# Sums of the mixes over two units instead of one, placed ahead of z, and three loads issued one unit sooner

## The chip, the cores and the metric

The kernel runs on one core of a Trainium2 chip. The metric is the device time in microseconds; lower is better. Times of the program are medians of several runs; the profile is one further execution.

## The reference, cut to what matters

```python
x_prev[:, 1:, :] = x[:, :-1, :]                 # x is (16, 2048, 256) fp32
xv = x * time_mix_v + x_prev * (1 - time_mix_v)
xr = x * time_mix_r + x_prev * (1 - time_mix_r)
v = xv.reshape(-1, 256) @ value_weight
r = xr.reshape(-1, 256) @ receptance_weight
out = (sigmoid(r) * v) @ output_weight          # (16, 2048, 256) fp32
```

The reference computes a key product too, but its output does not depend on it, and the kernel leaves it out. The weights are scaled with the time mixes beforehand, so that a mix is x + c * x_prev: one product with a coefficient per channel (`c_sb`) and one sum.

## The kernel before

**Units and pieces.** The 32,768 tokens are cut into 64 units of 512 tokens, four to a batch. A unit g is worked on with its channels on the partitions, as 1,024 elements per partition (two halves of the 256 channels, called ko 0 and ko 1, times 512 tokens). `pieces(u)` gives the two mixes of unit u: m = 0 for the receptance r, m = 1 for the value v. Tiles `mix` hold two units (an even one and the odd one behind it) with both mixes; there are three such tiles in turn.

**A loop over g.** The order on every engine is the order of the program text; nothing is reordered. In one pass for unit g:

- TensorE projects r of unit g into `psum_r` (`project`, L364, 4 matmuls), transposes tokens of a later unit as long as there are any (L269; from unit 34 on the transposed tokens come by DMA), projects v of unit g into `psum_v` (L364), and multiplies an earlier z with the output weight (L393, 8 matmuls). From unit 34 on the output of unit g - 2 stands between r and v; before, that of g - 1 stands behind v. `psum_v` has one buffer, so v of unit g + 1 waits until z of unit g has read it.
- ScalarE takes the sigmoid of r (L629), copies transposed tokens (L286) and outputs (L442), and from unit 34 on makes a part of the products (`scale_act`, L609).
- VectorE makes products (`scale`, L334), sums (`add`, L356), z = sigmoid * v (L668) and, once in four units, a shifted copy at the border of a batch (`wrap_slots`, L528).
- GpSimd makes the other half of the products (`scale_pool`, L344). By a dependency written by hand it starts only when the last sum of the list `sums[g]` has ended. It also issues the loads of x.

**Lists.** What is mixed when is written down ahead of the loop in lists by unit: `products[g]` ahead of the sums, `sums[g]` ahead of v and z, `held[g]` behind z, and `pooled[g]` for GpSimd, behind `sums[g]`. From unit 10 on (`PAIRS`) the products cover two units at once: ko 0 by VectorE at `products[w]` (or, for m = 1 from unit 34 on, by ScalarE one unit sooner), ko 1 by GpSimd at `pooled[w - 1]`, with w = u - 2 for m = 0 and w = u - 1 for m = 1, u being the even unit of the pair. The sums, however, are made unit by unit: of unit u, that of m = 0 is in `held[u - 2]` (from unit 8 on) and that of m = 1 in `sums[u - 1]`.

**Loads and stores.** The last six batches are cast to bf16 in DRAM by a load that GpSimd issues (`load`, L155 and L159) and then transposed by a DMA on SyncE's queue (`by_dma`, L251), three batches at a time, at units 27 and 39. `STAGE_AT` says in which unit loads 13, 14 and 15 are issued, behind GpSimd's product; each waits by hand for the transposition that was issued at unit 27. The transposition at unit 39 waits for these loads, and the stores of some units wait in SyncE's queue for them (`FIRST`, `WAITING`).

Of the kernel before, what the change touches and what calls it, by code (L numbers as in the profile page):

```python
# [15 lines left out]
def kernel(  # L16
# [32 lines left out]
    TU = UJ * P  # L49
# [12 lines left out]
    FIRST = {21: 27, 27: 39, 29: 39}  # L62
    WAITING = {23: 27, 25: 27, 31: 39, 33: 39, 35: 39}
    ZEROS_AT = 12
    STAGE_AT = {33: 13, 34: 14, 35: 15}
    GROUPS = [(2, 3), (4, 5, 6), (7, 8, 9), (10, 11, 12), (13, 14, 15)]
    HALVED = (12, 15)
    PAD = 16
# [4 lines left out]
    PAIRS = 10  # L73
# [63 lines left out]
    def zero_rows(b, k):  # L137
        rows = zeros[k * PAD : (k + 1) * PAD].rearrange("p (o c) -> p o c", o=1)
        nc.gpsimd.dma_start(
            out=x_both[b][k, :PAD].rearrange("p (h c) -> p h c", c=P),  # L140
            in_=rows.to_broadcast([PAD, KO, P]),
        )

    def load(b):
        if b < STAGED:
            x_bf[b] = xpool.tile([P, J, D], BF16, name="x_bf")
        if b < BYUNIT:
            for e in range(UB):
                nc.gpsimd.dma_start(
                    out=x_bf[b][:, e * UJ : (e + 1) * UJ, :], in_=unit_rows(x, b, e)[:, 0]  # L150
                )
            return
        if b in HALVED:
            return [
                nc.gpsimd.dma_start(out=x_bf[b][:, j : j + J // 2], in_=rows(b)[:, j : j + J // 2])  # L155
                for j in (0, J // 2)
            ]
        run = 8192 if b < LONG else 16384
        return nc.gpsimd.dma_start(out=x_bf[b], in_=rows(b), max_dma_last_dim=run)  # L159
# [339 lines left out]
    def tile_for(b):  # L499

        if b not in mix:
            mix[b] = mixpool.tile([P, 2, 2 * UJ, KO, P], BF16, name="mix")

    def pieces(g):

        b, e = divmod(g, UB)
        tile_for(g // 2)
        return [(b, m, e * TU, (e + 1) * TU) for m in range(2)]
# [68 lines left out]
    sums = {g: [] for g in range(-1, NU)}  # L577
# [4 lines left out]
    first = {}  # L582
    held[0].append(pieces(1)[1])
    pooled[0].append(pieces(1)[1])
    for u in range(2, NU):
        p0, p1 = pieces(u)
        if u - 1 <= AHEAD:
            sums[u - 1].append(p0)
        else:
            held[u - 2].append(p0)  # L590
        (held if u - 1 < AHEAD else sums)[u - 1].append(p1)
        first[u] = (u - 1 if u - 1 <= AHEAD else u - 2, u - 1)
# [24 lines left out]
    for g in range(NU - 1):  # L617
# [48 lines left out]
        n = TU // 2 if g == NU - 2 else TU  # L666
# [10 lines left out]
        if ZEROS_AT <= g < ZEROS_AT + len(pads):  # L677
            zero_rows(*pads[g - ZEROS_AT])
        if g in STAGE_AT:
            b = STAGE_AT[g]  # L680
            loads[b] = load(b)
# [40 lines left out]
```

## Time and profile before

| | |
|---|---|
| median of 3 runs | 200.42 us (200.24 to 200.9) |
| profiled execution, its own time | 201.01 us |
| span of the profile (first to last instruction) | 199.2 us |
| TensorE busy, of the span | 192.5 us, 97% |
| VectorE busy | 184.4 us, 93% |
| ScalarE busy | 177.0 us, 89% |
| GpSimd busy | 86.9 us, 44% |
| granted TensorE clock | 0.995 |

In the profile PE is TensorE's matmuls, PEld its weight loads, DVE VectorE, ACT ScalarE, POOL GpSimd and SP SyncE; a small q behind a name means the engine's queue, which issues DMAs. L356 is line 356 of the kernel. A row of the timeline gives start, duration, engine, line, operation, output and inputs, shapes and count; neighbouring equal instructions are merged into one row. In brackets stands how long the engine was idle before, and for whom.

Two successive VectorE rows overlap by about 0.08 us[...]. The distance from start to start, which is called the step below, is therefore what an instruction takes from the engine when the next one is ready.

### The profile page before, as it was taken

The page shows a single profiled execution, that of the slowest core. Times are in us where ns is not written, and L with a number is a line of the kernel's source. Part 1 is how long each engine was busy: PE and PEld are TensorE (multiplying, and loading weights), DVE is VectorE, ACT ScalarE, POOL GpSimd, SP SyncE. Part 2 cuts the span into 40 slices and gives each one's busy share as a digit, 9 for nine tenths or more (in the row PEclk, how much of TensorE's full clock was granted, in tenths as well). Part 3 has the DMA queues.
Part 4 walks back from the last instruction along what each step waited for, and adds up shares of the span by engine and source line. Part 5 has one row for each costly group of instructions (what it writes and reads, how often), then busy time and mean ns, then how long its engine had stood idle before and what let it go on. Part 6 is the DMA issues. An engine that isn't in the chain of part 4 may idle for free.

```text
span 199.2 us, 3758 instructions
## 1 busy us (share of the span) xinstructions
PE 192.5 (97%) x1368; PEld 123.5 (62%) x1368; DVE 184.4 (93%) x289; ACT 177.0 (89%) x197; POOL 86.9 (44%) x115
## 2 busy tenths in 40 slices
PE   8999999999999999999999999999999999999990
PEld 3555676666666666666666556666666666666660
DVE  0899999999999999999999999999999999999960
ACT  3699899999999999999999999999999999999970
POOL 1656452453675635524424366444444444444200
PEclk9999999999999999999999999999999999999998
DMA  5799999999999999999999999999999999999994
GB/s 177 203 187 215 215 280 275 278 282 274 286 312 332 285 285 331 296 268 211 296 250 290 367 276 207 209 280 295 198 238 346 416 421 400 409 399 407 409 392 177
DMA packets 37961, 58.13 MB, mean 292 GB/s; under 512 B 26068, under 2 KB 27448, under 8 KB 35128
## 3 DMA queue, kind: packets, MB, share of 16 engines
q1 hardware_dynamic: 33392, 41.34, 60.7%
q0 software_dynamic: 4400, 16.44, 41.6%
q8 instruction: 10, 0.16, 0.3%
q10 hardware_dynamic: 152, 0.13, 0.2%
q14 instruction: 7, 0.06, 0.1%
HBM read 34.34 MB, written 39.90 MB: 373 GB/s over the span
## 4 chain that ended last, share of the span: by engine, by line
PE 88%; ACT 4%; DMA 2%; issue 2%; DVE 1%; SPq 0%; DVEq 0%
PE psum_v L364 26%; PE psum_o L393 26%; PE psum_r L364 26%; PE ps_t L269 8%; DMA w_f<-n_receptance_weight_dram 2%; ACT xt_first L286 1%; ACT s_sb L629 1%; PE psum_r L378 1%; PE ps_t L393 1%; ACT mix L609 1%; ACT o_sb L442 1%; PE ps_t L364 0%; SPq L171 0%; DVE z_sb L668 0%; DVE mix L356 0%
## 5 line engine op out<-in xcount | busy, mean ns | idle before, releaser
L344 POOL TENSOR_SCALAR mix<-xt_both,c_sb 128x1024 bf16<-128x1024 bf16 (+1 forms) x55 | 61.3, 1114 | 84.7 <-DVE mix L356 82.8
L356 DVE TENSOR_TENSOR mix<-mix,xt_both 128x1024 bf16<-128x1024 bf16 x112 | 77.4, 701 | 1.4
L668 DVE TENSOR_TENSOR z_sb<-s_sb,psum_v 128x1024 bf16<-128x1024 bf16 (+1 forms) x64 | 76.7, 1200 | 1.9 <-PE psum_v L364 0.8
L364 PEld LDWEIGHTS <-w_bf 128*128 128x128 bf16 x516 | 49.0, 98 | 38.7 <-DVE mix L356 0.5
L629 ACT ACTIVATE s_sb<-psum_r 128x1024 bf16<-128x1024 f32 x63 | 65.2, 1035 | 6.2 <-PE psum_r L364 6.0
L364 PE MATMUL psum_v<-mix,w_bf 128*128 128x512 bf16 (+1 forms) x256 | 65.3, 377 | 0.1
L364 PE MATMUL psum_r<-mix,w_bf 128*128 128x512 bf16 (+1 forms) x252 | 64.2, 377 | 0.0
L393 PE MATMUL psum_o<-wo_bf,z_sb 128*128 128x256 bf16 x486 | 63.4, 273 | 0.2 <-DVE z_sb L668 0.2
L393 PEld LDWEIGHTS <-z_sb 128*128 128x128 bf16 x512 | 51.7, 103 | 18.2 <-DVE z_sb L481 0.7
L442 ACT COPY o_sb<-psum_o 128x1024 f32<-128x1024 f32 x50 | 51.2, 1024 | 5.0 <-PE psum_o L393 5.0
L286 ACT COPY xt_both<-ps_t 128x1024 bf16<-128x1024 bf16 x32 | 32.8, 1036 | 0.0
L269 PEld LDWEIGHTS <-x_bf 128*128 128x128 bf16 x304 | 19.7, 98 | 8.9 <-DMA x_bf<-in_x_dram 1.5
L269 PE MATMUL ps_t<-ident,x_bf 128*128 128x128 bf16 x304 | 22.7, 219 | 0.3 <-DMA x_bf<-in_x_dram 0.3
L334 DVE TENSOR_SCALAR mix<-xt_both,c_sb 128x1024 bf16<-128x1024 bf16 (+1 forms) x47 | 21.1, 458 | 0.0
L609 ACT ACTIVATE mix<-xt_both,c_sb 128x1024 bf16<-128x1024 bf16 x14 | 16.3, 1161 | 0.0
L356 DVE TENSOR_TENSOR mix<-mix,xt_first 128x1024 bf16<-128x1024 bf16 x15 | 10.6, 713 | 0.1
L442 ACT COPY x_bf<-psum_o 128x1024 f32<-128x1024 f32 x10 | 10.2, 1015 | 0.0
L334 DVE TENSOR_SCALAR mix<-xt_first,c_sb 128x512 bf16<-128x512 bf16 x22 | 6.5, 348 | 0.3 <-ACT xt_first L279 0.2
L286 ACT COPY xt_first<-ps_t 128x1024 bf16<-128x1024 bf16 x6 | 6.2, 1027 | 0.0
L159 POOL DMA_DIRECT2D x_bf<-in_x_dram x8 | 5.7, 712 | 0.0
L528 POOL COPY xt_first<-xt_first 128x254 bf16<-128x254 bf16 x5 | 2.0, 395 | 6.6 <-DVE mix L356 6.6
L344 POOL TENSOR_SCALAR mix<-xt_first,c_sb 128x512 bf16<-128x512 bf16 x6 | 4.1, 689 | 0.7 <-DVE mix L356 0.2
(70 smaller groups left out, 54.0 us busy)
## 6 DMA issues: line engine op xcount, KB each, us to landing
out_dram<-o_sb SPq DMA_DIRECT2D x24, 1024.0 KB, 14.1
x_bf<-in_x_dram POOLq DMA_DIRECT2D x8, 1024.0 KB, 20.6
x_natural<-in_x_dram POOLq DMA_DIRECT2D x4, 1024.0 KB, 13.3
out_dram<-x_bf SPq DMA_DIRECT2D x4, 1024.0 KB, 13.1
x_natural<-in_x_dram POOLq DMA_DIRECT2D x4, 512.0 KB, 15.2
x_bf<-in_x_dram POOLq DMA_DIRECT2D x6, 256.0 KB, 6.1
out_dram<-x_bf SPq DMA_DIRECT2D x6, 256.0 KB, 4.2
o_sb<-in_x_dram SPq DMA_DIRECT2D x4, 256.0 KB, 4.0
```

The source lines that it names most:

```text
L159: return nc.gpsimd.dma_start(out=x_bf[b], in_=rows(b), max_dma_last_dim=run)
L269: nc.tensor.transpose(out=ps[:, jj], in_=src[:, jj, ko * P : (ko + 1) * P], identity=idn)
L286: nc.scalar.copy(out=xt[b][:, j0 : j0 + UJ], in_=ps)
L334: nc.vector.tensor_scalar(out=mixed(piece)[:, :, ko], in0=tokens(piece, 0, ko), scalar1=c_sb[:, m, ko : ko + 1], scalar2=None, op0=ALU.mult,)
L344: op = nc.gpsimd.tensor_scalar(out=mixed(piece)[:, :, 1], in0=tokens(piece, 0, 1), scalar1=c_sb[:, m, 1:2], scalar2=1.0, op0=ALU.mult, op1 ...
L356: return nc.vector.tensor_tensor(out=mixed(piece), in0=mixed(piece), in1=tokens(piece, 1), op=ALU.add)
L364: nc.tensor.matmul(out=ps[:, mo, :], lhsT=w_bf[:, m, ko, mo * P : (mo + 1) * P], rhs=mixed((b, m, e * TU + lo, e * TU + hi))[:, :, ko], st ...
L393: nc.tensor.matmul(out=ps[:, j, :], lhsT=slot[:, ko, j], rhs=wo_bf[:, ko, :], start=(ko == 0), stop=(ko == KO - 1),)
L442: nc.scalar.copy(out=o[:, j0 : j0 + UJ, :], in_=ps)
L609: nc.scalar.activation(out=mixed(piece)[:, :, ko], in_=tokens(piece, 0, ko), func=ACT.Copy, scale=c_sb[:, m, ko : ko + 1],)
L629: nc.scalar.activation(out=s_sb, in_=ps_r, func=ACT.Sigmoid)
L668: nc.vector.tensor_tensor(out=z_sb[:, :, c : c + n], in0=s_sb[:, :, c : c + n], in1=ps_v[:, :, c : c + n], op=ALU.mult,)
```

## The change

The sums of m = 0 and of m = 1 are made for both units of a pair in one instruction each, 2,048 elements per partition in place of 1,024, from unit 10 on. For a pair with even unit u, that of m = 0 moves to `sums[u - 2]` and that of m = 1 to `sums[u - 1]`; both stand ahead of z, and nothing is put into `held` any more. The products keep their places. Loads 13, 14 and 15 are issued in units 32, 33 and 34.

```diff
-    STAGE_AT = {33: 13, 34: 14, 35: 15}
+    STAGE_AT = {32: 13, 33: 14, 34: 15}
...
     for u in range(2, NU):
         p0, p1 = pieces(u)
+        if u >= PAIRS:
+            if u % 2 == 0:
+                for n, (b, m, lo, hi) in ((2, p0), (1, p1)):
+                    sums[u - n].append((b, m, lo, hi + TU))
+            first[u] = (u - 2, u - 1)
+            continue
         if u - 1 <= AHEAD:
             sums[u - 1].append(p0)
         else:
             held[u - 2].append(p0)
         (held if u - 1 < AHEAD else sums)[u - 1].append(p1)
         first[u] = (u - 1 if u - 1 <= AHEAD else u - 2, u - 1)
```

## The prediction

> **What bounds the kernel now.** I read the page first, then the waits, then the timeline of single engines around the units that the change touches.
>
> ```profile
> PE 192.5 (97%) x1368; PEld 123.5 (62%) x1368; DVE 184.4 (93%) x289; ACT 177.0 (89%) x197; POOL 86.9 (44%) x115
> ...
> PE   8999999999999999999999999999999999999990
> ...
> DVE  0899999999999999999999999999999999999960
> ```
>
> TensorE is busy in every slice but the first and the last. The table of stretches gives it 70.00 of the 70 us from 42 to 112 and 75.00 of the 75 from 112 to 187, and the chain of waits puts 88% of the span on PE. Its pace is that of the matmuls: 8 output matmuls take 0.87 us in the chain, and the middle units (to 33) repeat every 3.05 us, the late ones (from 34) every 2.60, three times 0.87. So VectorE, though 93% busy, can give nothing back by being shorter. It can only take: v of the next unit needs z of this one out of `psum_v`. What counts is how late z runs.
>
> ```profile
> DVE z_sb L668 <- PE psum_v L364: 0.8, 4, 0.2
> ```
>
> In the list of waits, z has waited only 0.8 us for v in all. By the timeline z starts 0.11 us after v's modelled end at the earliest (that is z on time); the bound for lateness I read at unit 6, where z ran until 32.82 and v of unit 7 started at 32.87, the only place between units 5 and 33 where it slipped (by 0.11 us). So v may start 0.05 us behind z's end. Late units then allow a z that is 0.2 us later than on time (2.60 - 1.03 for v - 1.22 for z - 0.05 - 0.11 = 0.19), middle ones 0.64.
>
> **Unit 8, where the double sums begin.** VectorE's rows:
>
> ```profile
> 34.73 1.22 DVE L668 TENSOR_TENSOR z_sb<-s_sb,psum_v 128x1024 bf16<-128x1024 bf16 x1
> 35.86 0.79 DVE L356 TENSOR_TENSOR mix<-mix,xt_both 128x1024 bf16<-128x1024 bf16 x1
> 36.57 1.00 DVE L334 TENSOR_SCALAR mix<-xt_both,c_sb 128x512 bf16<-128x512 bf16 x3
> 37.49 0.68 DVE L356 TENSOR_TENSOR mix<-mix,xt_both 128x1024 bf16<-128x1024 bf16 x1
> 38.10 1.21 DVE L668 TENSOR_TENSOR z_sb<-s_sb,psum_v 128x1024 bf16<-128x1024 bf16 x1
> 39.23 0.70 DVE L356 TENSOR_TENSOR mix<-mix,xt_both 128x1024 bf16<-128x1024 bf16 x1
> ...
> 39.98 0.47 DVE L334 TENSOR_SCALAR mix<-xt_both,c_sb 128x1024 bf16<-128x1024 bf16 x1
> 40.56 0.69 DVE L356 TENSOR_TENSOR mix<-mix,xt_both 128x1024 bf16<-128x1024 bf16 x1
> ```
>
> and TensorE's v of units 8 and 9:
>
> ```profile
> 36.36 1.03 PE L364 MATMUL psum_v<-mix,w_bf 128*128 128x512 bf16 x4
> ...
> 39.41 1.03 PE L364 MATMUL psum_v<-mix,w_bf 128*128 128x512 bf16 x4
> ```
>
> VectorE has no gap here: z of unit 8 (38.10) is already 0.6 us later than on time, ends at 39.31, and v of unit 9 starts at 39.41. Only 0.05 us is left. The row at 37.49 is the m = 1 sum of unit 9; the row at 39.23, behind z, is the m = 0 sum of unit 10, which the change doubles and puts ahead of z. The last two rows show a second thing: a sum that reads the product just ahead of it starts 0.10 us after that product's end (40.56 against 39.98 + 0.475), not 0.08 before it.
>
> **The skill on the two operations.** "VectorE: DVE Perf Modes", section "The perf-mode tier table", gives 1,224 ns to a tensor_tensor of 2,048 bf16 elements in SBUF; the same page says that an instruction's fixed cost is paid once per instruction. The trace has no such row, but its sum of 1,024 takes 0.68 us with a step of 0.60. Two steps without any saving are 1.21; I take 1.22 us of duration and, 0.08 less as in the other rows, a step of 1.13 (bounds 1.13 to 1.21). The saving is 0.07 us a pair, not half an instruction. "SBUF — State Buffer", section "Who interferes with whom", says that VectorE and GpSimd share a port pair, and that whoever has it blocks the other for the whole instruction. The trace agrees:
>
> ```profile
> 81.29 1.13 DVE L356 TENSOR_TENSOR mix<-mix,xt_both 128x1024 bf16<-128x1024 bf16 x1
> ...
> 80.75 1.13 POOL L344 TENSOR_SCALAR mix<-xt_both,c_sb 128x1024 bf16<-128x1024 bf16 x1
> ```
>
> GpSimd ended at 81.88, the sum at 82.42, 0.54 later; the sum at 35.86 also ended 0.54 after GpSimd (36.11). So a blocked sum has 0.14 of its 0.68 us behind it and does the rest when GpSimd is done. For a blocked product of 0.475 I estimate 0.335 after GpSimd. The forecast goes by the trace's numbers.
>
> **Part 1: 108 single sums become 54 double ones.** They occupy 54 x (2 x 0.60 - 1.13) = 4 us less of VectorE. Worth to the end: nothing, since TensorE sets it.
>
> **Part 2: the order at unit 8.** A step of 1.13 goes in ahead of z: 38.10 becomes 39.23, z ends at 40.45, v of unit 9 starts at 40.50 instead of 39.41: 1.1 us lost. Queued behind that v are output 8 and everything TensorE does later, with no idle time to win it back. With the other end of the step it is 1.2. At unit 9 VectorE does z 1.13, border copy 0.14, product 0.48, gap 0.10, double sum 1.13: 2.98 a unit, under 3.05, so unit 10 starts without another wait, though barely.
>
> **Part 3: the middle units.** Each has z 1.13, product 0.48, gap 0.10, double sum 1.13 = 2.84 us, in every fourth unit 0.14 more, against 3.05. VectorE catches up by unit 14. Cost 0; what hides it is the 0.21 us by which TensorE is slower.
>
> **Part 4: the late units.** Now every sum starts behind a GpSimd product that itself waits for the sum before it; in the kernel before, the sum held behind z filled that time.
>
> ```profile
> 118.92 1.22 DVE L668 TENSOR_TENSOR z_sb<-s_sb,psum_v 128x1024 bf16<-128x1024 bf16 x1
> ...
> 121.09 0.68 DVE L356 TENSOR_TENSOR mix<-mix,xt_both 128x1024 bf16<-128x1024 bf16 x1
> ...
> 119.12 1.12 POOL L344 TENSOR_SCALAR mix<-xt_both,c_sb 128x1024 bf16<-128x1024 bf16 x1 [0.80 <-DVE mix L356]
> ...
> 121.87 1.12 POOL L344 TENSOR_SCALAR mix<-xt_both,c_sb 128x1024 bf16<-128x1024 bf16 x1 [0.58 <-DVE mix L356]
> ```
>
> GpSimd follows the sum's end by 0.17 us in odd units (118.95 to 119.12) and 0.10 in even ones (121.77 to 121.87), and takes 1.12. One pair, from the start of the m = 1 sum in an odd unit (0): it ends at 1.22; GpSimd's m = 0 product runs 1.39 to 2.51. z starts at 1.13, and VectorE's product could start at 2.26, but is blocked, and ends at 2.51 + 0.335 = 2.84. The m = 0 double sum follows at 2.94, ends at 4.16; GpSimd's m = 1 product runs 4.26 to 5.38; the next m = 1 sum needs it and starts 0.04 later (a sum at 69.10 began 0.02 after GpSimd's end; others 0.09): 5.42. TensorE needs 5.20. The allowed lateness of 0.2 is spent where the pace drops at unit 34, since VectorE needs 2.84 there. From unit 35 to 61 there are 13 pairs: 13 x 0.22 = 2.9 us. Without the blocking the product ends at 2.74 and the round is 5.32: 13 x 0.12 = 1.5. ScalarE's part of the m = 1 product ends earlier than GpSimd's and costs nothing.
>
> **Part 5: the loads.** Four DMA issues (0.56, 0.56 and two in 1.10 us on GpSimd) move up one unit. Load 13 goes behind GpSimd's product at unit 32 (110.49 to 111.61); the transposition it waits for landed at 110.61, so it need not wait, and there is 1.8 us of cover before the product at 113.94. Load 15's 1.10 us fit between two products (1.4 us). In SyncE's queue the held stores and the second transposition (133.90 to 151.13) come up to 2.6 us sooner, but GpSimd first needs its result at 155.45. Beside the two stores at 110.70 the loads may land later; those 4.3 us cover it. Cost and gain 0.
>
> **Sum.** 1.1 + 2.9 = 4.0 us: span 199.2 to 203.2, the profiled execution, which lies 1.8 over its span and 0.6 over the median, to about 205.0, the median 200.42 to 204.4.
>
> **Rivals.** (a) Only unit 8 costs: the late round fits into 5.20, by handovers shorter than I took or an unblocked product. 201.5, or up to 203.3 with half of it; for it, the round rests on gaps of 0.04 to 0.17 us; against it, even the unblocked round is 5.32. Chance 0.26. (b) Faster: VectorE, not TensorE, paces the late units (it is busy 74.64 of 75 us), TensorE's modelled ends hiding the waits. Then 14 pairs save 2 x 0.07 each, and the sum's gap and waits behind GpSimd must not take it back: 2.0 less, 1.1 lost at unit 8, 199.5 (200.42 - 2.0 + 1.1). It decides once an unseen wait of over 0.1 us a late unit exists; against it, 2.60 is three times the 0.87 that TensorE needs where VectorE has gaps. Chance 0.05. (c) Within 0.3%, about what a measurement of this kernel can tell from no change (0.6 us): z at unit 8 finds slack I don't see. 0.05. (d) Over 205.6: handovers of 0.1 (0.06 more a pair, twice over), or double sums that lose their two elements a cycle; the latter I give little, as the access pattern keeps its form and only a count doubles. 0.06. My forecast, 203.3 to 205.6, keeps 0.58.
>
> Range 201.3 to 205.6, with 0.82 inside. Slower 0.90, same 0.05, faster 0.05.
>
> **What would show it.** 54 sums at 1.22 us; v of unit 9 about 1.1 us later, with a wait of PE for z; v in the middle still every 3.05; late units 5.4 a pair, VectorE waiting for POOL ahead of every odd sum; the loads issued near 113, 116 and 119. A late pair at 5.20 proves part 4 wrong; v of unit 9 near 39.4 proves part 2 wrong.

## The result and the profile after

The changed kernel takes 203.07 us (median of 6 runs, 202.58 to 204.66) against 200.44 (6 runs, 200.06 to 201.69): a ratio of 1.013, 95% interval 1.0086 to 1.0174, or 2.6 us (1.7 to 3.5). The forecast was 204.4, range 201.3 to 205.6. The profiled execution took 202.58 us, its span is 200.8. It is the fastest of the six, while the profiled execution of the kernel before (201.01) was slower than its median; so the two spans differ by only 1.6 us.

The page of the changed kernel, the same rows as before the change:

```profile
PE 194.6 (97%) x1368; PEld 122.7 (61%) x1368; DVE 182.2 (91%) x235; ACT 177.0 (88%) x197; POOL 86.9 (43%) x115
...
PE   8999999899999999999999999999999999999992
...
DVE  0999999999999999998999999999999999999952
```

VectorE has 54 instructions less and is busy 2.2 us less (part 1 had 4 us, counted in steps; what makes the difference was not worked out); the program is slower all the same. TensorE's row shows the lost time only as one 8 instead of a 9, in the eighth slice (35.1 to 40.2 us); its other waits are too short for a slice of 5 us. They stand in the list of waits:

```profile
PEld L364 <- issue: 3.4, 14, 1.0
...
PE psum_v L364 <- DVE z_sb L674: 0.9, 1, 0.9
```

Behind the colon are the total, the count and the longest. The weight loads of the projections sat idle 14 times: once for 1.0 us, at unit 9 (where the matmul's own wait for z, 0.9, is in the second row), and 13 times for 0.18 in the late units. No such row stood there before.

**Unit 8.** VectorE and TensorE in the timeline of the changed kernel:

```profile
36.31 1.00 DVE L334 TENSOR_SCALAR mix<-xt_both,c_sb 128x512 bf16<-128x512 bf16 x3
37.23 1.82 DVE L356 TENSOR_TENSOR mix<-mix,xt_both 128x1024 bf16<-128x1024 bf16 x2
38.96 1.21 DVE L674 TENSOR_TENSOR z_sb<-s_sb,psum_v 128x1024 bf16<-128x1024 bf16 x1
...
36.10 1.03 PE L364 MATMUL psum_v<-mix,w_bf 128*128 128x512 bf16 x4
...
40.23 1.02 PE L364 MATMUL psum_v<-mix,w_bf 128*128 128x512 bf16 x4 [0.91 <-DVE z_sb L674]
```

The row at 37.23 is two sums merged by the view, the single one of unit 9 and the first double one. z ends at 40.17 (38.96 + 1.21), v of unit 9 starts at 40.23. From v of unit 8 to v of unit 9 it is 4.13 us, where it was 3.05: 1.08 lost.

**A late pair.** VectorE, GpSimd and TensorE's v projections:

```profile
130.57 1.21 DVE L674 TENSOR_TENSOR z_sb<-s_sb,psum_v 128x1024 bf16<-128x1024 bf16 x1
131.70 0.52 DVE L334 TENSOR_SCALAR mix<-xt_both,c_sb 128x1024 bf16<-128x1024 bf16 x1
132.32 1.22 DVE L356 TENSOR_TENSOR mix<-mix,xt_both 128x2048 bf16<-128x2048 bf16 x1
133.46 1.21 DVE L674 TENSOR_TENSOR z_sb<-s_sb,psum_v 128x1024 bf16<-128x1024 bf16 x1
134.79 1.23 DVE L356 TENSOR_TENSOR mix<-mix,xt_both 128x2048 bf16<-128x2048 bf16 x1
...
130.82 1.12 POOL L344 TENSOR_SCALAR mix<-xt_both,c_sb 128x1024 bf16<-128x1024 bf16 x1 [1.43 <-DVE mix L356]
133.64 1.12 POOL L344 TENSOR_SCALAR mix<-xt_both,c_sb 128x1024 bf16<-128x1024 bf16 x1 [1.70 <-DVE mix L356]
...
131.96 1.03 PE L364 MATMUL psum_v<-mix,w_bf 128*128 128x512 bf16 x4
...
134.73 1.02 PE L364 MATMUL psum_v<-mix,w_bf 128*128 128x512 bf16 x4
```

The sum of the odd unit starts right behind GpSimd's product: 134.79 against GpSimd's end at 134.76 (133.64 + 1.12). The sum of the even unit, at 132.32, starts 0.10 behind VectorE's product. That product takes 0.52 in place of 0.48; GpSimd works until 131.94, and the product ends at 132.22, 0.28 later. In VectorE's steps a pair has z 1.13, product 0.62, sum 1.14, z 1.33 and sum 1.14. Against an undisturbed z (1.13) and product (0.58, with the gap behind it) that is 0.20 of waiting for GpSimd ahead of the odd sum and 0.04 in the product; without them the steps come to 5.12. v at 134.73 starts 0.06 behind the end of z (134.67), as at unit 9. v starts at intervals of 2.60 and 2.77 in turn, 5.37 a pair.

**The end.** The stretches of the last microseconds (of each stretch: its length; busy us of PE, PEld, DVE, ACT and POOL; clock, the DMA engines' busy share and GB/s), first before the change, then after it:

```profile
185.00:190.00 5.00, 5.00 (x37) 3.37 (x35) 4.68 (x8) 4.50 (x8) 0.36 (x1) 1.00 1.03 409
190.00:195.00 5.00, 3.99 (x31) 2.46 (x29) 3.09 (x6) 3.22 (x8) 0.00 (x0) 1.00 1.01 384
```

```profile
185.00:190.00 5.00, 4.99 (x36) 3.32 (x33) 4.78 (x6) 4.85 (x6) 1.70 (x2) 1.00 0.73 294
190.00:195.00 5.00, 4.85 (x38) 3.34 (x35) 2.77 (x4) 4.00 (x7) 0.00 (x0) 1.00 0.75 293
```

Before, the DMA engines were full to the end; after, they have slack from 185 us on. The three smallest of the last stores, of 128 KB each, took longer from issue to landing before than after (the last figure of the row is their median in us; first before, then after):

```profile
out_dram<-x_bf SPq DMA_DIRECT2D x3, 128.0 KB, 3.0
```

```profile
out_dram<-x_bf SPq DMA_DIRECT2D x3, 128.0 KB, 2.0
```

So before, stores were still queued up when the last output came. From the end of the last compute row to the end of the span it was 4.6 us (194.6 to 199.2), and is 3.2 (197.6 to 200.8). These are single executions, and the one with 4.6 was 0.6 us over the median of its kernel; what the end is worth is read from the runs below. The prediction had not looked there.

### The profile page after: what moved, and what is told of

It reads as the page before. It is cut to its first block, busy times and chain, and to the rows that moved or that the text cites. A ratio compares the mean times of both kernels' runs of the same rounds, so it can differ in the third digit from the quotient of the medians.

```text
span 200.8 us, 3703 instructions
## 1 busy us (share of the span) xinstructions
PE 194.6 (97%) x1368; PEld 122.7 (61%) x1368; DVE 182.2 (91%) x235; ACT 177.0 (88%) x197; POOL 86.9 (43%) x115
## 4 chain that ended last, share of the span: by engine, by line
PE 77%; DVE 13%; issue 3%; DMA 2%; SPq 1%; POOL 1%; ACT 1%; DVEq 0%; POOLq 0%
PE psum_v L364 24%; PE psum_o L393 23%; PE psum_r L364 23%; PE ps_t L269 5%; DVE mix L356 5%; DVE z_sb L674 4%; DVE mix L334 4%; DMA w_f<-in_value_weight_dram 2%; SPq L171 1%; PE ps_t L393 1%; ACT s_sb L635 1%; PE ps_t L364 0%; POOL x_bf L159 0%; POOL mix L344 0%; DVE w_bf L565 0%
## 5 line engine op out<-in xcount | busy, mean ns | idle before, releaser
L356 DVE TENSOR_TENSOR mix<-mix,xt_both 128x2048 bf16<-128x2048 bf16 (+1 forms) x58 | 68.9, 1190 | 6.0 <-DVE mix L334 0.5
L334 DVE TENSOR_SCALAR mix<-xt_both,c_sb 128x1024 bf16<-128x1024 bf16 (+1 forms) x47 | 21.9, 475 | 0.0
```

Of the source, the lines that this page charges most:

```text
L334: nc.vector.tensor_scalar(out=mixed(piece)[:, :, ko], in0=tokens(piece, 0, ko), scalar1=c_sb[:, m, ko : ko + 1], scalar2=None, op0=ALU.mult,)
L356: return nc.vector.tensor_tensor(out=mixed(piece), in0=mixed(piece), in1=tokens(piece, 1), op=ALU.add)
```

## The experiments

TensorE's pace is read from the starts of v in the timeline, so that the start of the program and its end are left out of it; "end" is the time from the end of the last compute row to the end of the span. Both come from one profile of each kernel. Ratios are to the kernel before, run on the same chip.

| kernel | v of unit 7 to v of unit 62, us | unit 8 to 10 | unit 33 to 62 | end, us | ratio (95%) |
|---|---|---|---|---|---|
| before | 155.11 | 6.09 | 75.44 | 4.6 | 1 |
| changed | 158.36 | 7.17 | 77.61 | 3.2 | 1.013 (1.0086 to 1.0174) |
| double sums alone | 158.38 | 7.17 | 77.63 | 3.2 | 1.0088 (1.0055 to 1.012) |
| loads alone | 155.12 | 6.09 | 75.44 | 3.2 | 0.9956 (0.9933 to 0.998) |
| double sums, units 10 to 33 | 156.19 | 7.17 | 75.44 | 3.2 | 1.0008 (0.9981 to 1.0034) |
| double sums from unit 34 | 158.11 | 6.09 | 78.25 | 3.2 | 1.0101 (1.0054 to 1.0149) |
| GpSimd a unit sooner | 157.65 | 7.17 | 76.90 | 3.2 | 1.0079 (1.0048 to 1.011) |
| the same, doubled from unit 20 | 156.90 | 6.09 | 76.93 | 3.2 | 1.0033 (1.0007 to 1.0059) |
| before, five stores left out | 155.12 | 6.09 | 75.44 | 3.0 | 0.993 (0.9905 to 0.9955) |
| changed, five stores left out | 158.51 | 7.17 | 77.77 | 3.1 | 1.0121 (1.007 to 1.0172) |
| first double sum behind z | 158.38 | 7.14 | 77.67 | 3.2 | 1.0122 (1.0069 to 1.0175) |

**1. The two parts of the change, each alone.**

The double sums alone are the changed kernel with

```diff
-    STAGE_AT = {32: 13, 33: 14, 34: 15}
+    STAGE_AT = {33: 13, 34: 14, 35: 15}
```

> The double sums alone, loads 13 to 15 in units 33 to 35 as in the kernel before. If the loads' move costs and gains nothing (my part 5), the time is that of the changed kernel, 203.1 us, v of unit 9 slips by 1.1 us and late pairs take 5.36 to 5.37 us. If it was the sooner loads that shortened the end of the changed kernel (4.6 us from the last compute row to the end of the span before, 3.2 after), the end is 4.3 us or more again and the time about 204.2.

and the loads alone the kernel before with

```diff
-    STAGE_AT = {33: 13, 34: 14, 35: 15}
+    STAGE_AT = {32: 13, 33: 14, 34: 15}
```

> The loads' move alone, single sums. If it costs and gains nothing: 200.4 us, within 0.3%, with a GpSimd wait of up to 1.5 us for the first transposition at unit 32 that delays nobody. If sooner loads let the stores drain sooner: 199.3 us, the end behind the last compute row 1.1 us shorter or more.

Measured: the double sums alone cost TensorE the same 3.3 us, and their end is 3.2 us long with the loads at their old place. So in the changed kernel the end would be as short without the sooner loads. The ratio, 1.0088, lies under both expectations (1.013 and 1.019); its interval overlaps that of the changed kernel, so whether the sooner loads cost something beside double sums is not shown. The loads alone leave TensorE's pace as it was and are 0.44% faster (0.2 to 0.67%), 0.9 us, with an end of 3.2 us. Each of the two, then, is enough to take the drain off the end, and together they take it off once. The stretch of the loads-alone kernel in which the compute ends:

```profile
190.00:195.00 5.00, 3.90 (x31) 2.38 (x28) 3.00 (x6) 3.14 (x7) 0.00 (x0) 1.00 0.80 306
```

The DMA engines are busy 0.80 there, where they were at 1.01. The stores that wait behind the second transposition in SyncE's queue start 1.6 us sooner, as their rows before the change and in this kernel show:

```profile
151.18 2.15 SPq L411 DMA_DIRECT2D out_dram<-o_sb  x3
```

```profile
149.61 2.14 SPq L411 DMA_DIRECT2D out_dram<-o_sb  x3
```

This kernel beats both others.

**2. Early and late units apart.** Both are the changed kernel with the loads at their old place and a narrower condition for the double sums.

```diff
-        if u >= PAIRS:
+        if PAIRS <= u < 34:
```

> Double sums for units 10 to 33 only, single ones from 34, loads as before. Both theories expect v of unit 9 to slip by 1.1 us and every late pair to take 5.20 us, so that the last compute row ends 1.1 us later. If lost compute time comes out in full at the end: 201.5 us. If the stores' drain sets the end of the kernel before and covers about 1.4 us of lost compute: 200.4 to 200.8 us, with the end behind the last compute row about 1.1 us shorter.

```diff
-        if u >= PAIRS:
+        if u >= 34:
```

> Double sums from unit 34 only, loads as before. No slip at unit 9; late pairs take 5.36 to 5.37 us, which is 13 x 0.165 = 2.1 us more by unit 61. In full at the end: 202.5 us. With about 1.4 us of it covered by the stores' drain: 201.1 us. If the late slip comes from the lateness that unit 8 left behind and not from the round of sums and GpSimd products: late pairs at 5.20 and 200.4 us.

Measured: with the early units alone TensorE loses 1.08 us at unit 9 and nothing else, and the time does not change (1.0008): the lost microsecond comes back at the end, which gets shorter. From unit 10 to 33 it is 70.09 us, as before the change. With the late units alone the pairs take 5.37 us, so they do not come from a lateness inherited from unit 8. But TensorE lost 3.0 us, not the 2.1 that was expected: v of units 33 to 35 comes 0.8 us late in all. In unit 32, as in unit 8, the list has a single sum and the first double one; that this makes the 0.8 is likely and was not tested. The time, 1.0% (2.0 us), is 1 us less than TensorE's loss.

**3. Is the round of sums and GpSimd products what makes the late pairs long?** The changed kernel with GpSimd's products from unit 36 on a unit sooner:

```diff
-                pooled[w - 1].append(group)
+                pooled[w - (2 if u >= 36 else 1)].append(group)
```

> The changed kernel with GpSimd's products of the pairs from unit 36 on made one unit sooner; all else equal. If the late pairs are long because every sum waits for a GpSimd product that waits for the sum before it, that round is cut: VectorE alone needs 4 x 1.13 + 0.52 + 0.10 and a little blocking, 5.1 to 5.2, so the late pairs fall from 5.365 to 5.20 us and v of unit 62 comes 2.1 us sooner. If the shared port or the sum's wait for VectorE's own product makes the round, they stay at 5.3 us or more. The slip of 1.1 us at unit 9 stays in both.

Measured: late pairs of 5.27 us, between the two expectations. GpSimd's products a unit sooner recover 0.10 of the 0.17 us a pair. VectorE's rows in this kernel, and one of GpSimd:

```profile
132.37 1.22 DVE L674 TENSOR_TENSOR z_sb<-s_sb,psum_v 128x1024 bf16<-128x1024 bf16 x1
133.51 0.48 DVE L334 TENSOR_SCALAR mix<-xt_both,c_sb 128x1024 bf16<-128x1024 bf16 x1
134.09 1.23 DVE L356 TENSOR_TENSOR mix<-mix,xt_both 128x2048 bf16<-128x2048 bf16 x1
135.24 1.22 DVE L674 TENSOR_TENSOR z_sb<-s_sb,psum_v 128x1024 bf16<-128x1024 bf16 x1
136.37 1.34 DVE L356 TENSOR_TENSOR mix<-mix,xt_both 128x2048 bf16<-128x2048 bf16 x1
137.63 1.22 DVE L674 TENSOR_TENSOR z_sb<-s_sb,psum_v 128x1024 bf16<-128x1024 bf16 x1
...
135.51 1.12 POOL L344 TENSOR_SCALAR mix<-xt_both,c_sb 128x1024 bf16<-128x1024 bf16 x1 [1.86 <-DVE mix L356]
```

No sum waits for a GpSimd product here, and the steps from 132.37 to 137.63 add up to 5.26. Two of them are longer than the bare instruction: the product with the gap behind it (0.58 for 0.40), because the sum reads it at once, and the odd sum (1.26 for 1.13). That sum starts at 136.37, while GpSimd works until 136.63, and ends at 137.71, 1.08 behind GpSimd: it is blocked, as the sums in the prediction were. Without the blocking the steps come to 5.13, which is under TensorE's 5.20. So the experiment takes one delay by GpSimd out of the round and puts a smaller one in; VectorE's own work, in this order, fits. A late unit with neither delay was not run.

**4. Can the double sums be had for nothing?** The same with the double sums from unit 20 on:

```diff
-        if u >= PAIRS:
+        if u >= 20:
...
-                pooled[w - 1].append(group)
+                pooled[w - (2 if u >= 36 else 1)].append(group)
```

> The same, and the double sums begin at unit 20, where z is on time, instead of unit 10; loads sooner as in the changed kernel. If units 8 and 34 to 61 are all that the double sums cost, TensorE's pace is that of the kernel before from unit 7 to 62 (155.1 us) and the time that of the loads' move alone, 0.4% under the kernel before. If double sums carry a further cost in the middle units, it is longer by that.

Measured: no, not in this form. The first double sum costs 0.29 us at unit 19 (v 3.34 behind that of unit 18), units 34 and 35 another 0.55 (in unit 32 GpSimd has two products to make there; that this is the reason was not tested), and the late pairs 0.07 each: 1.8 us of TensorE, 0.3% of the time (0.07 to 0.59%).

**5. Does the drain of the stores set the end?** Five stores of 1 MB are left out, in both kernels:

```diff
-            for pair in kept.pop(g, []):
-                store(nc.sync, *pair)
+            kept.pop(g, [])
```

> The kernel before without the five stores of 1 MB that wait in SyncE's queue for loads (pairs of units 23, 25, 31, 33 and 35 are not written out). Compute is untouched. If the drain of the stores sets the end of the kernel before, the time falls by about 1 us, to a ratio of about 0.995, and the end behind the last compute row to about 3.2 us. If compute sets it, the ratio is 1.000.

> The changed kernel without the same five stores. Its stores have drained before its end, so the time should stay that of the changed kernel, and its distance to the kernel before without these stores should be the whole 3.2 us that TensorE loses, 1.6%. If stores still held its end, it falls by about 1 us as the other does.

Measured: the kernel before gets 0.7% faster (0.45 to 0.95%, 1.4 us) with an untouched TensorE pace; the changed one stays at 1.2%. Their distance is then 1.9%, 3.8 us, for 3.4 us of TensorE between them; the intervals are wide enough for the difference. So the end of the kernel before is the stores' drain, 0.9 to 1.9 us behind what the compute needs, and about the first microsecond that a change takes from TensorE is hidden. By the ratios, the seven kernels with double sums and all stores are slower by 0.6 to 1.5 us less than TensorE's loss; a closer figure the runs do not give.

**6. What it is at unit 8 that costs.** The changed kernel with one sum moved:

```diff
-                    sums[u - n].append((b, m, lo, hi + TU))
+                    (held if (u, m) == (PAIRS, 0) else sums)[u - n].append((b, m, lo, hi + TU))
```

> The changed kernel, but the first double sum (m = 0 of units 10 and 11) is made behind z of unit 8 instead of ahead of it. If the place ahead of z is what costs at unit 8, v of unit 9 starts 3.05 us after that of unit 8 again, and v of unit 62 comes 1.1 us sooner. If the cost is that the sum of unit 11 is made a unit sooner on a VectorE that has no gap there, the slip only moves by one unit: v of unit 9 on time, v of unit 10 about 1 us late, v of unit 62 unchanged.

Measured: v of unit 9 is on time and that of unit 10 is late instead:

```profile
39.30 1.03 PE L364 MATMUL psum_v<-mix,w_bf 128*128 128x512 bf16 x4
...
43.39 1.02 PE L364 MATMUL psum_v<-mix,w_bf 128*128 128x512 bf16 x4 [0.88 <-DVE z_sb L674]
```

4.09 us in place of 3.05, and the same 158.38 us to unit 62. The place ahead of z only says which unit pays; what costs is that the sum of 512 tokens more is made earlier, in a stretch where VectorE has no gap.

## Why the prediction was right, and where its terms were off

- **TensorE sets the pace, and VectorE can only take.** Shown: VectorE's busy time fell, the time rose, and where VectorE kept up (units 10 to 33) nothing changed to 0.01 us.
- **Part 1.** The double sum takes 1.22 to 1.23 us, as estimated and as the Trainium skill's "VectorE: DVE Perf Modes", section "The perf-mode tier table", has it (1,224 ns).
- **Part 2.** 1.1 us forecast, 1.08 measured, at the unit named. The reason given, the place ahead of z, was half of it: behind z it costs the same, one unit later.
- **Part 3.** Nothing forecast, nothing measured.
- **Part 4.** The mechanism was right, its size too large: 5.42 us a pair forecast, 5.37 measured; 13 x 0.22 = 2.9 against 2.17. The mis-sized term is the one estimate without a row of its own, the blocked product: 0.335 us behind GpSimd's end, measured 0.28. The missing 0.055 is the whole difference. The rival that the pairs fit into 5.20 fell. The rows and the one experiment on the mechanism agree that the excess hangs on GpSimd: the wait for it (0.20 a pair) and a blocked product (0.04) in the changed kernel, a blocked sum (0.13) where its products come sooner.
- **Part 5 failed.** It said that the loads cost and gain nothing. Alone they gain 0.9 us. The step that was wrong took the output stores as hidden: it asked who waits for the loads and the transposition, found 4.3 us of cover, and did not ask when the last store lands. It also said that GpSimd need not wait at unit 32, as the transposition's row ended at 110.61. That row is the issue, not the landing. The view of the DMA issues before the change gives 13.7 us from issue to landing:

```profile
xt_both<-x_natural SPq DMA_TRANSPOSE x2, 13.7
```

  From the issue at 99.00 that is 112.7, and not 110.61. In the changed kernel the row ended at 111.41, and GpSimd waited on:

```profile
99.48 11.93 SPq L251 DMA_TRANSPOSE xt_both<-x_natural  x1
...
114.04 0.56 POOL L159 DMA_DIRECT2D x_natural<-in_x_dram  x1 [1.49 <-DMA xt_both<-x_natural]
```

  The skill's "Perfetto Trace Analysis", section "Summary: the profiler window per engine type", says so of both kinds of DMA in its table: the row leaves out the movement of the data. GpSimd's next product started at 114.69, 0.18 behind the end of the sum that it waits for (114.51), as in the other odd units, so the wait cost nothing.
- **The sum.** 1.1 + 2.9 = 4.0 forecast; TensorE lost 1.08 + 2.17 = 3.25. In the profiles the end gave back 1.4 and v of unit 7 came 0.3 us sooner, so that the spans differ by 1.6. In the runs 2.6 us (1.7 to 3.5) came out, with the double sums alone 1.8 (1.1 to 2.4). The term that was missing from the sum is the drain. It made the forecast too high, as the size of part 4 did; the two errors did not cancel.
- **The number alone would not have decided.** 203.07 lies under the stretch that the forecast kept for itself (203.3 to 205.6) and in that of rival (a), by which unit 8 costs and the late units nothing, or up to half. The late pairs of 5.37 us decide against that rival: TensorE lost 2.17 of the 2.9 us there. That its number fits is a coincidence, since neither side had the drain.
- **The faster rival** fell: VectorE had 54 instructions less, and no late pair came in under 5.20.

## What to carry to other kernels

Merging two instructions saved only 0.07 us here (a step of 1.13 for two of 0.60), and it moves half of the work earlier; on an engine without gaps that delay is paid once at the start, and a chain that alternates between two engines loses the work that used to fill its gaps. Before costing a change by the busiest compute engine alone, look at what the DMA engines do behind the last compute instruction. Here a drain hid about the first microsecond of a loss, and moving three loads, which relieved it, was worth more than the double sums, which only cost.

## What the runs showed of the hardware that was not expected

- A VectorE product that GpSimd held up ended 0.28 us after GpSimd did, a sum of 1,024 elements 0.54 (read before the change), a sum of 2,048 elements 1.08. For both sums that is their own duration less 0.14 us; for the product (0.48) it is less 0.20.
- A sum that read the VectorE product just ahead of it started 0.58 us after the product did (133.51 to 134.09), one that did not 0.40 (151.86 to 152.26 before the change): 0.18 us for a gap of 0.10 in place of an overlap of 0.08. In the late units the double sums put every VectorE product in that place.
- The transposition's row lasted 11.93 us, and the instruction that waited for its data went on 14.6 us after its issue.
